# Normalising attention outputs in place of probabilities, and preparing the last branch's weights ahead

## The chip, the core and the metric

The kernel runs on one core of a Trainium2 chip. A core has five engines that run side by side, each with a queue that is worked off in order: TensorE (PE, matrix products into PSUM), VectorE (DVE), ScalarE (ACT), GpSimd (POOL) and SyncE (SP, which here issues nearly all DMAs). They meet through semaphores. The metric is the time of one execution in microseconds (us) on the device.

## What is computed

One layer on 512 tokens of width 1024: a gated feed-forward block (inner width 2816), a mixing block, and a second feed-forward block. The mixing block has two attention branches of 8 heads with 64 columns each. Branch b ("moba") attends to all keys up to the query, since with two blocks of 256 keys its choice of blocks leaves none out. Branch a ("dsa") attends to the 128 best keys by a separate score. Cut to what matters:

```python
h = h + 0.5 * swiglu(rmsnorm(h, g1), w_gu1, w_down1)
u = rmsnorm(h, g_mix)
# per head and query block, branch a; branch b is alike without the selection
logits = q @ k.T * scale + bias
p = softmax(logits)                  # exp(l - max) / sum
out = p @ v
...
mixed = sigmoid(g_a) * (out_a @ w_branch_dsa) + sigmoid(g_b) * (out_b @ w_branch_moba)
h = h + mixed @ w_out
h = h + 0.5 * swiglu(rmsnorm(h, g2), w_gu2, w_down2)
```

## The kernel before

Everything is float32. For matrix products each operand is split into a high part (rounded to the matrix engine's own 32-bit format) and a low part (the rest), and each product is made of three: high x high, high x low, low x high (`mm3`, lines 118 to 120). Activations lie transposed, 128 features on the partitions and 512 tokens along a row.

*Weights* come in units of up to 128 x 1024. `wunit` issues one DMA from SP into a tile `raw`; ScalarE makes the high part `whi` (line 108), and another engine the low part `wlo` (line 109), GpSimd but for the very first units. There are three tiles of each kind, so a load waits until the split of three units earlier is done, and a high part until TensorE has used the unit of three earlier.

*Order.* TensorE's order is written out by hand in the program. On the other engines a planner orders the instructions at build time by their place in the program and its own estimate of when each can run; those in a block with raised priority (`HURRY`) go first. From then on each queue is fixed.

*Attention* runs over 32 steps for each branch: 8 heads times 4 blocks of 128 queries, step i being head i // 4, block i % 4, with 128 to 512 keys. In a step `logits` makes the scores in PSUM (`s`), VectorE adds the bias and takes the extremum (line 589), ScalarE takes the exponential and its sum along a row (`log_exp`, line 75), VectorE makes the reciprocal of the sum (line 592) and scales the probabilities (line 593). Two steps later `turn` transposes them on TensorE, 128 x 128 at a time, into a PSUM tile `pt`, of which there are two (line 601); ScalarE copies the high part out (line 609) and VectorE the low part (line 610). After each head `values` multiplies with v into PSUM `o` and adds the two halves into `osum` (lines 626, 627); after the second head of a pair `osum` is split into high and low and is one of the four tiles of `outs`. Between these TensorE works on the filler: the projections of other heads and the gates, one k-step of three matmuls at each `yield`. Branch b's attention runs first, from about 420 to 536 us, then its output projection and the choice of the 128 keys (on VectorE), then branch a's attention, about 604 to 722 us.

*The last branch* (the loop over c below attention's end) makes, for each of 8 tiles of the output, the product of `oa` with `wb_a` (12 matmuls), times the gate (line 747), plus branch b's part (line 748), and splits the sum into high and low (lines 145, 146). Gate tiles 0 to 6 are made in attention's filler, tile 7 in the loop's first round. Behind the loop come two units of `w_out` side by side on all eight `mixed` tiles (`ps2`), then the other six.

Of the kernel before, what the change touches and what calls it, by code (L numbers as in the profile page):

```python
# [14 lines left out]
ALU = mybir.AluOpType  # L15
# [35 lines left out]
def block_kernel(ctx, tc, x, gains, wgu1, wd1, w_in, w_v, wb_a, wb_b, w_out, wgu2, wd2, rel_bias, onehot, out):  # L51
# [55 lines left out]
    def wsplit(raw, hi, lo, eng=nc.gpsimd):  # L107
        nc.scalar.activation(hi, raw, AF.Copy)  # L108
        eng.tensor_sub(lo, raw, f32(hi))  # L109

    def wunit(src):
        raw, hi, lo = wtiles(src.shape[1])
        nc.sync.dma_start(raw, src)
        wsplit(raw, hi, lo)
        return tuple(a.rearrange("p (k c) -> p k c", c=P) for a in (hi, lo))

    def mm3(pt, wh, wl, xh, xl, start, stop):
# [235 lines left out]
        while late:  # L353
            late.pop(0)[1]()

    def unit(src, xs, post):
        p = mmps()
        for _ in mmk(p, wunit(src), xs):
            tick()
            yield  # L360
        post(p)
# [62 lines left out]
    for low in lows:  # L424
        for e in range(2):
            nc.gpsimd.memset(f32(low)[HALF[1 - e], e, :], 0.0)
    turns = [0]

    def k_post(p, gain, dst):

# [110 lines left out]
            nc.gpsimd.memset(f32(pts[i][j])[:, 1408:1536], 0.0)  # L541

    sums = {}

    def attention(br, pairs, outs, extra):

        sel = br == 0
        bias, prob, tms, osum = {}, {}, {}, {}

        def table(hd):  # L550
            if hd < 8:
# [19 lines left out]
        def logits(i):  # L571
            if i >= 32:
                return
            hd, qt = divmod(i, 4)
            if qt == 1:
                table(hd + 1)
            e = hd % 2
            (q, f, _), (k, kl), _ = pairs[hd // 2]
            W = P * (qt + 1)
            N = max(W, 256)  # L580
            p = sps()
            qb = q[:, e, qt * P:(qt + 1) * P]
            nc.tensor.matmul(p[:, 0:N], qb, k[:, e, 0:N], start=True, stop=False)
            nc.tensor.matmul(p[:, 0:N], qb, kl[:, e, 0:N], start=False, stop=True)
            addend(i + 1)
            pe = tms.pop(i)
            st = T("st", 8, (P, 4))
            with tc.high_priority(HURRY):
                sums[i] = nc.vector.tensor_tensor_reduce(  # L589
                    out=pe, in0=p[:, 0:W], in1=pe, scale=f[:, 2 * qt + e:2 * qt + e + 1], scalar=3e38, op0=ALU.add, op1=ALU.min, accum_out=st[:, 0:1])  # L590
                log_exp(pe, pe, AF.Exp, bias=st[:, 0:1], scale=-1.0, accum_out=st[:, 1:2])
                nc.vector.reciprocal(st[:, 2:3], st[:, 1:2])
                nc.vector.tensor_scalar(pe, pe, st[:, 2:3], None, op0=ALU.mult)  # L593
            prob[i] = pe

        def turn(i):
            hd, qt = divmod(i, 4)
# [14 lines left out]
        def values(hd):  # L612
# [12 lines left out]
            with tc.high_priority(HURRY):  # L625
                nc.scalar.activation(ot[0:DH, :], po[DH:P, :], AF.Copy)
                nc.vector.tensor_add(osum[0][e * DH:(e + 1) * DH, :], po[0:DH, :], ot[0:DH, :])
            if e == 1:
                outs.append(split(pair_a(), osum[0]))

        table(0)
# [5 lines left out]
        for i in range(32):  # L637
            logits(i + 2)
            yield 1
            turn(i)  # L640
            yield 1
            if i % 4 == 1 and i > 4:
                values(i // 4 - 1)
            if extra and i % EVERY == 0:
                extra.pop(0)()
            yield 1
# [29 lines left out]
            keep[gi] = g1  # L676
        return proj(U_G + gi, post)

    def branch(wb, c, o, post):
        return unit(wb[c], o, post)  # L680

    def opened(gi):
        g1 = gates.pop(gi)
# [55 lines left out]
    run(fill)  # L739
    flush()  # L740
    mixed = []
    for c in range(KD):
        if c + GATES < KD:
            run(gate(c + GATES, gates))
        g1 = opened(c)
        ma = tmp()
        run(branch(wb_a, c, oa, lambda p: nc.vector.tensor_mul(ma, p, g1)))
        nc.vector.tensor_add(ma, ma, mixb[c])
        if c < 3:
            m = T("kqk"[c], 2, (P, 2, S), F32R)  # L750
# [10 lines left out]
        xs2.append(norm_tile(c, G_N2, ss3))  # L761

    ps2 = [mmps() for _ in range(2)]
    together([mmk(p, wunit(w_out[c]), mixed) for c, p in enumerate(ps2)])
    for c, p in enumerate(ps2):
        wout_post(c, p)
    for c in range(2, KD):
# [64 lines left out]
```

## Time and profile before

| | |
|---|---|
| median of 3 runs | 1164.97 us (1162.73 to 1166.91) |
| profiled execution | 1167.82 us, of which the span 1166.0 us |
| mean granted TensorE clock | 0.992 |
| TensorE, VectorE, ScalarE, GpSimd busy | 98%, 60%, 40%, 46% of the span |
| DMA | 109.59 MB, 94 GB/s on the mean |

The span goes from the first to the last instruction. Busy shares are over the whole span; the stages differ much, and a share of VectorE of 60% is made of the feed-forward blocks with less and of attention with more. TensorE's matmuls overlap (one of 512 columns is shown with some 0.39 us and they start 0.23 us apart), so a busy TensorE says that it has work, not how fast that goes. Where the clock is granted in part, its mean over a stretch is given as a share of full speed.

### The profile page before, as it was taken

To read this page: it belongs to the slowest core of one execution; us is meant where nothing else is said; L and a number is where in the kernel's file an instruction comes from. 1 tells how busy PE (TensorE), PEld (TensorE's weight loads), DVE (VectorE), ACT (ScalarE), POOL (GpSimd) and SP (SyncE) were. 2 spreads that over 40 slices of the span, in tenths; PEclk is the share of its full clock that TensorE was granted. 3 is DMA by queue.
4 is the path that set the end of the run, shared out by engine and by line. 5 is a ranking of instruction groups with operands and counts; after the bars stand their busy time and mean duration, and the time that the engine had idled before them with its cause. 6 is when DMAs were issued, how large, how long until landed. Compare 5 with 4: busy or idle time off the path is not lost.

```text
span 1166.0 us, 14074 instructions
## 1 busy us (share of the span) xinstructions
PE 1141.1 (98%) x5356; PEld 949.4 (81%) x5356; DVE 701.4 (60%) x1075; ACT 467.3 (40%) x757; POOL 532.8 (46%) x284
## 2 busy tenths in 40 slices
PE   9999999999999999999998899999999999999998
PEld 7878888888888888778887778788888888888887
DVE  5863166513556579899979986664754156622551
ACT  6322132222334668757247656433332132222221
POOL 3444444444444655753453422444444444444442
PEclk9999999999999999999999999999999999999999
DMA  7232222332323221221241311322333222332222
GB/s 235 93 111 91 99 100 91 97 102 91 99 81 110 97 76 55 92 68 69 89 137 46 100 55 35 106 104 73 108 102 98 92 107 91 94 105 91 97 84 91
DMA packets 38171, 109.59 MB, mean 94 GB/s; under 512 B 4214, under 2 KB 8664, under 8 KB 38104
## 3 DMA queue, kind: packets, MB, share of 16 engines
q1 hardware_dynamic: 37960, 108.67, 28.2%
q8 instruction: 42, 0.69, 0.2%
q14 instruction: 25, 0.20, 0.1%
q10 hardware_dynamic: 144, 0.02, 0.0%
HBM read 106.54 MB, written 2.14 MB: 93 GB/s over the span
## 4 chain that ended last, share of the span: by engine, by line
PE 83%; DVE 9%; ACT 3%; issue 3%; POOL 1%; DMA 0%; SPq 0%; POOLq 0%; ACTq 0%; DVEq 0%
PE mm L120 20%; PE mm L118 20%; PE mm L119 20%; PE s L118 7%; PE s L119 7%; PE s L120 7%; DVE l L566 1%; DVE l L589 1%; POOL wlo L109 1%; DVE l L593 1%; DVE pt L610 1%; PE pt L601 1%; ACT l L75 1%; DVE low L453 1%; PE o L620 1%
## 5 line engine op out<-in xcount | busy, mean ns | idle before, releaser
L109 POOL TENSOR_TENSOR wlo<-raw,whi 128x1024 fp32r<-128x1024 f32 (+2 forms) x199 | 466.2, 2344 | 541.4 <-ACT whi L108 536.4
L108 ACT ACTIVATE whi<-raw 128x1024 fp32r<-128x1024 f32 (+2 forms) x207 | 205.0, 992 | 520.5 <-PE mm L119 289.6
L118 PE MATMUL mm<-x,whi 128*128 128x512 f32 x632 | 253.0, 400 | 0.7 <-ACT whi L108 0.7
L120 PE MATMUL mm<-x,wlo 128*128 128x512 f32 x632 | 247.6, 392 | 0.0
L119 PE MATMUL mm<-x,whi 128*128 128x512 f32 x632 | 247.3, 391 | 0.0
L119 PE MATMUL mm<-a,whi 128*128 128x512 f32 (+1 forms) x462 | 178.7, 387 | 0.3
L118 PE MATMUL mm<-a,whi 128*128 128x512 f32 (+1 forms) x462 | 178.7, 387 | 0.0
L120 PE MATMUL mm<-a,wlo 128*128 128x512 f32 (+1 forms) x462 | 178.5, 386 | 0.0
L120 PEld LDWEIGHTS mm<-x,wlo 128*128 128x128 f32 x632 | 119.1, 188 | 25.9 <-DVE wlo L109 0.4
L118 PEld LDWEIGHTS mm<-x,whi 128*128 128x128 f32 x632 | 119.5, 189 | 23.1 <-ACT whi L108 1.5
L118 PE MATMUL s<-x,whi 128*128 128x512 f32 x352 | 137.0, 389 | 0.6 <-ACT tmp L75 0.6
L120 PE MATMUL s<-x,wlo 128*128 128x512 f32 x352 | 137.0, 389 | 0.0
L119 PE MATMUL s<-x,whi 128*128 128x512 f32 x352 | 136.9, 389 | 0.0
L119 PEld LDWEIGHTS mm<-x,whi 128*128 128x128 f32 x632 | 119.5, 189 | 21.0 <-issue 0.5
L271 DVE SCALAR_TENSOR_TENSOR h<-mm,h 128x512 f32<-128x512 f32 (+1 forms) x49 | 33.3, 680 | 165.3 <-PE mm L120 165.3
L262 DVE TENSOR_TENSOR tmp<-tmp,tmp 128x512 f32<-128x512 f32 x44 | 99.0, 2250 | 29.6 <-ACT tmp L75 29.4
L146 DVE TENSOR_TENSOR a<-tmp,a 128x512 fp32r<-128x512 f32 x49 | 88.5, 1807 | 31.9 <-ACT a L145 31.8
L119 PEld LDWEIGHTS mm<-a,whi 128*128 128x128 f32 x462 | 86.9, 188 | 18.7 <-DVE a L146 1.1
L118 PEld LDWEIGHTS mm<-a,whi 128*128 128x128 f32 x462 | 86.9, 188 | 17.6
L120 PEld LDWEIGHTS mm<-a,wlo 128*128 128x128 f32 x462 | 86.8, 188 | 17.6
L118 PEld LDWEIGHTS s<-x,whi 128*128 128x128 f32 x352 | 66.1, 188 | 14.6 <-ACT tmp L75 1.0
L120 PEld LDWEIGHTS s<-x,wlo 128*128 128x128 f32 x352 | 66.1, 188 | 13.8
(167 smaller groups left out, 1417.0 us busy)
## 6 DMA issues: line engine op xcount, KB each, us to landing
raw<-in_ffn_w_gu_dram SPq DMA_DIRECT2D x84, 512.0 KB, 3.5
raw<-in_w_in_dram SPq DMA_DIRECT2D x35, 512.0 KB, 3.5
raw<-in_ffn_w_down_dram SPq DMA_DIRECT2D x32, 512.0 KB, 3.5
raw<-in_ffn_w_down_dram SPq DMA_DIRECT2D x16, 384.0 KB, 3.0
bias<-fd SPq DMA_DIRECT2D x16, 256.0 KB, 3.5
raw<-in_w_v_dram SPq DMA_DIRECT2D x8, 512.0 KB, 3.4
raw<-in_w_out_dram SPq DMA_DIRECT2D x8, 512.0 KB, 3.5
h<-in_x_dram SPq DMA_DIRECT2D x8, 256.0 KB, 4.6
```

The source lines that it names most:

```text
L75: op = after([group["load"]], lambda: nc.scalar.activation(*a, **k))
L108: nc.scalar.activation(hi, raw, AF.Copy)
L109: eng.tensor_sub(lo, raw, f32(hi))
L118: nc.tensor.matmul(pt, wh, xh, start=start, stop=False)
L119: nc.tensor.matmul(pt, wh, xl, start=False, stop=False)
L120: nc.tensor.matmul(pt, wl, xh, start=False, stop=stop)
L146: nc.vector.tensor_sub(lo, src, f32(hi))
L262: nc.vector.tensor_mul(g1, g1, s)
L271: nc.vector.scalar_tensor_tensor(h[c][:, b], pd, 0.5, h[c][:, b], op0=ALU.mult, op1=ALU.add)
L453: nc.vector.scalar_tensor_tensor(low[h1, e, :], y[h1, :], g, f32(k)[h1, e, :], op0=ALU.mult, op1=ALU.subtract)
L566: nc.vector.scalar_tensor_tensor(tms[i], b, inv, work[:, WOFF[qt]:WOFF[qt] + W], op0=ALU.mult, op1=ALU.add)
L589: sums[i] = nc.vector.tensor_tensor_reduce(out=pe, in0=p[:, 0:W], in1=pe, scale=f[:, 2 * qt + e:2 * qt + e + 1], scalar=3e38, op0=ALU.add, ...
```

## The change

The probabilities are no longer divided by their sums. The sums of the eight steps of a pair of heads are collected in a tile `tot` of 128 x 8 (queries on the partitions). After the seventh step's `turn` (i % 8 == 6), `norms` takes the reciprocals of all eight columns, transposes them on TensorE (a 128 x 128 tile, zero but for eight columns), copies the eight rows out with the query order turned round, writes them to DRAM as a row and reads them back, each head's 512 values spread over the 64 partitions of its half. When both heads' outputs stand in `osum`, it is multiplied by that tile, on GpSimd, or on VectorE for the last pair of branch a.

In the last branch gate 7 is made ahead of the loop. The units of `wb_a` and the first two of `w_out` are prepared by `fetch`, two units ahead in the program's order, with the low part on VectorE in place of GpSimd. The other six units of `w_out` stay as they were.

```diff
--- before.py
+++ after.py
@@ -108,10 +108,10 @@
         nc.scalar.activation(hi, raw, AF.Copy)
         eng.tensor_sub(lo, raw, f32(hi))
 
-    def wunit(src):
+    def wunit(src, eng=nc.gpsimd):
         raw, hi, lo = wtiles(src.shape[1])
         nc.sync.dma_start(raw, src)
-        wsplit(raw, hi, lo)
+        wsplit(raw, hi, lo, eng)
         return tuple(a.rearrange("p (k c) -> p k c", c=P) for a in (hi, lo))
 
     def mm3(pt, wh, wl, xh, xl, start, stop):
@@ -353,9 +353,9 @@
         while late:
             late.pop(0)[1]()
 
-    def unit(src, xs, post):
+    def unit(src, xs, post, w=None):
         p = mmps()
-        for _ in mmk(p, wunit(src), xs):
+        for _ in mmk(p, w or wunit(src), xs):
             tick()
             yield
         post(p)
@@ -424,7 +424,7 @@
     for low in lows:
         for e in range(2):
             nc.gpsimd.memset(f32(low)[HALF[1 - e], e, :], 0.0)
-    turns = [0]
+    turns = [0, 0]
 
     def k_post(p, gain, dst):
 
@@ -541,11 +541,15 @@
             nc.gpsimd.memset(f32(pts[i][j])[:, 1408:1536], 0.0)
 
     sums = {}
+    recips = [cp.tile([P, P], F32, name=f"recip{i}") for i in range(2)]
+    rows_d = [dr.tile([8, P], F32, name=f"row{i}") for i in range(2)]
+    for r1 in recips:
+        nc.gpsimd.memset(r1, 0.0)
 
     def attention(br, pairs, outs, extra):
 
         sel = br == 0
-        bias, prob, tms, osum = {}, {}, {}, {}
+        bias, prob, tms, osum, tot, inv_s = {}, {}, {}, {}, {}, {}
 
         def table(hd):
             if hd < 8:
@@ -585,13 +589,31 @@
             addend(i + 1)
             pe = tms.pop(i)
             st = T("st", 8, (P, 4))
+            if i % 8 == 0:
+                tot[hd // 2] = T("tot", 2, (P, 8))
+            s1 = tot[hd // 2][:, i % 8:i % 8 + 1]
             with tc.high_priority(HURRY):
                 sums[i] = nc.vector.tensor_tensor_reduce(
                     out=pe, in0=p[:, 0:W], in1=pe, scale=f[:, 2 * qt + e:2 * qt + e + 1], scalar=3e38, op0=ALU.add, op1=ALU.min, accum_out=st[:, 0:1])
-                log_exp(pe, pe, AF.Exp, bias=st[:, 0:1], scale=-1.0, accum_out=st[:, 1:2])
-                nc.vector.reciprocal(st[:, 2:3], st[:, 1:2])
-                nc.vector.tensor_scalar(pe, pe, st[:, 2:3], None, op0=ALU.mult)
+                log_exp(pe, pe, AF.Exp, bias=st[:, 0:1], scale=-1.0, accum_out=s1)
             prob[i] = pe
+
+        def norms(pr):
+
+            r1 = recips[turns[1] % 2]
+            row = rows_d[turns[1] % 2]
+            turns[1] += 1
+            nc.vector.reciprocal(r1[:, 0:8], tot.pop(pr))
+            p = tps()
+            nc.tensor.transpose(p[:, 0:P], r1, ident)
+            o = p[0:8, P - 1:P]
+            rw = T("rw", 2, (8, P))
+            nc.scalar.activation(rw, bass.AP(o.tensor, o.offset, [list(o.ap[0]), [-1, P]]), AF.Copy)
+            nc.sync.dma_start(row, rw)
+            rb = inv_s[pr] = T("rb", 2)
+            for e in range(2):
+                a = row[4 * e:4 * e + 1, :]
+                nc.sync.dma_start(rb[HALF[e], :], bass.AP(a.tensor, a.offset, [[0, DH], [1, S]]))
 
         def turn(i):
             hd, qt = divmod(i, 4)
@@ -626,6 +648,8 @@
                 nc.scalar.activation(ot[0:DH, :], po[DH:P, :], AF.Copy)
                 nc.vector.tensor_add(osum[0][e * DH:(e + 1) * DH, :], po[0:DH, :], ot[0:DH, :])
             if e == 1:
+                eng = nc.vector if sel and hd == 7 else nc.gpsimd
+                eng.tensor_mul(osum[0], osum[0], inv_s.pop(hd // 2))
                 outs.append(split(pair_a(), osum[0]))
 
         table(0)
@@ -638,6 +662,8 @@
             logits(i + 2)
             yield 1
             turn(i)
+            if i % 8 == 6:
+                norms(i // 8)
             yield 1
             if i % 4 == 1 and i > 4:
                 values(i // 4 - 1)
@@ -676,8 +702,8 @@
             keep[gi] = g1
         return proj(U_G + gi, post)
 
-    def branch(wb, c, o, post):
-        return unit(wb[c], o, post)
+    def branch(wb, c, o, post, w=None):
+        return unit(wb[c], o, post, w)
 
     def opened(gi):
         g1 = gates.pop(gi)
@@ -739,12 +765,24 @@
     run(fill)
     flush()
     mixed = []
+
+    ahead = [wb_a[c] for c in range(KD)] + [w_out[c] for c in range(2)]
+    ready = []
+
+    def fetch():
+        if ahead:
+            ready.append(wunit(ahead.pop(0), nc.vector))
+
+    for c in range(GATES, KD):
+        run(gate(c, gates))
+    for _ in range(2):
+        fetch()
     for c in range(KD):
-        if c + GATES < KD:
-            run(gate(c + GATES, gates))
         g1 = opened(c)
         ma = tmp()
-        run(branch(wb_a, c, oa, lambda p: nc.vector.tensor_mul(ma, p, g1)))
+        w = ready.pop(0)
+        run(branch(wb_a, c, oa, lambda p: nc.vector.tensor_mul(ma, p, g1), w))
+        fetch()
         nc.vector.tensor_add(ma, ma, mixb[c])
         if c < 3:
             m = T("kqk"[c], 2, (P, 2, S), F32R)
@@ -761,7 +799,7 @@
         xs2.append(norm_tile(c, G_N2, ss3))
 
     ps2 = [mmps() for _ in range(2)]
-    together([mmk(p, wunit(w_out[c]), mixed) for c, p in enumerate(ps2)])
+    together([mmk(p, w, mixed) for p, w in zip(ps2, ready)])
     for c, p in enumerate(ps2):
         wout_post(c, p)
     for c in range(2, KD):
```

## Rows read from the trace of the kernel before

**Rows 1.** The page's first part: busy time, share of the span, instructions.

```profile
PE 1141.1 (98%) x5356; PEld 949.4 (81%) x5356; DVE 701.4 (60%) x1075; ACT 467.3 (40%) x757; POOL 532.8 (46%) x284
```

**Rows 2.** TensorE's waits: instruction and releaser, us in total, times, longest.

```profile
PE pt L601 <- DVE pt L610: 12.0, 10, 2.6
...
PE mm L118 <- DVE tmp L747: 1.5, 1, 1.5
PE mm L120 <- POOL wlo L109: 1.3, 1, 1.3
```

**Rows 3.** Busy us of each engine, sum of the six stretches named below.

```profile
sum 79.00, PE 64.31 PEld 50.98 DVE 76.41 ACT 55.38 POOL 33.76; mean PE 10.72 PEld 8.50 DVE 12.73 ACT 9.23 POOL 5.63
```

**Rows 4.** The same stretches, lines 592 and 593 alone; then their groups in attention.

```profile
sum 79.00, DVE 3.05; mean DVE 0.51
...
sum 79.00, DVE 10.13; mean DVE 1.69
...
L592 DVE RECIPROCAL st<-st 128x1 f32<-128x1 f32 x64 | 10.0, 157 | 9.0 <-ACT l L75 8.4
...
L593 DVE TENSOR_SCALAR l<-l,st 128x512 f32<-128x512 f32 x16 | 7.7, 483 | 0.2
```

**Rows 5.** Stretches: engines' busy us (instructions), granted clock, DMA share, GB/s.

```profile
529.00:538.00 9.00, 8.33 (x55) 7.84 (x54) 8.19 (x22) 7.05 (x14) 2.32 (x1) 0.81 0.11 32
664.00:676.00 12.00, 9.37 (x39) 7.70 (x38) 9.32 (x21) 6.78 (x16) 2.23 (x3) 0.72 0.18 66
751.00:763.00 12.00, 9.25 (x28) 6.76 (x26) 9.75 (x8) 3.79 (x5) 5.51 (x3) 0.72 0.32 108
```

**Rows 6.** Timeline, 674 to 688 us: start, duration, instruction, [idle before, releaser].

```profile
675.63 2.40 POOL L109 TENSOR_TENSOR wlo<-raw,whi 128x1024 fp32r<-128x1024 f32 x1 [6.57 <-ACT whi L108]
675.70 2.36 DVE L415 TENSOR_TENSOR fq<-fq 128x8 f32<-128x8 f32 x1
...
685.64 2.54 DVE L593 TENSOR_SCALAR l<-l,st 128x256 f32<-128x256 f32 x1
685.66 2.36 POOL L109 TENSOR_TENSOR wlo<-raw,whi 128x1024 fp32r<-128x1024 f32 x1 [0.67 <-ACT whi L108]
```

**Rows 7.** Timeline of the last branch, 735 to 752 us.

```profile
735.12 0.39 PE L118 MATMUL mm<-a,whi 128*128 128x512 f32 x1
...
737.84 0.39 PE L118 MATMUL mm<-a,whi 128*128 128x512 f32 x1
...
739.07 0.69 DVE L146 TENSOR_TENSOR q<-tmp,q 128x512 fp32r<-128x512 f32 x1 [0.70 <-ACT q L145]
...
739.68 0.68 DVE L747 TENSOR_TENSOR tmp<-mm,tmp 128x512 f32<-128x512 f32 x1
...
742.79 0.68 DVE L747 TENSOR_TENSOR tmp<-mm,g 128x512 f32<-128x512 f32 x1
...
749.39 2.39 POOL L109 TENSOR_TENSOR wlo<-raw,whi 128x1024 fp32r<-128x1024 f32 x1 [2.24 <-PE mm L119]
...
749.72 2.61 DVE L748 TENSOR_TENSOR tmp<-tmp,a 128x512 f32<-128x512 f32 x1
```

**Rows 8.** Groups by line (busy us, mean ns); a DMA (KB, us to landing).

```profile
L438 POOL TENSOR_TENSOR tmp<-tmp,tmp 128x512 fp32r<-128x512 f32 x8 | 10.9, 1361 | 0.8 <-ACT tmp L436 0.4
...
L109 DVE TENSOR_TENSOR wlo<-raw,whi 128x512 fp32r<-128x512 f32 x8 | 5.5, 684 | 0.6 <-ACT whi L108 0.6
...
bias<-fd SPq DMA_DIRECT2D x16, 256.0 KB, 3.5
```

**Rows 9.** Timeline, 472 to 474 us: a reciprocal and the transposes after it.

```profile
472.61 0.17 DVE L592 RECIPROCAL st<-st 128x1 f32<-128x1 f32 x1 [0.55 <-ACT l L75]
...
473.36 0.49 PE L601 MATMUL pt<-ident,l 128*128 128x128 f32 x3
```

**Rows 10.** Timeline: a weight load on SP and the first use of it.

```profile
422.08 0.33 SPq L113 DMA_DIRECT2D raw<-in_w_in_dram  x1
...
444.10 1.04 ACT L108 ACTIVATE whi<-raw 128x1024 fp32r<-128x1024 f32 x1
```

## The prediction

> **What bounds the kernel now.** I read the engines' shares first: TensorE is busy 98% of the span [rows 1]. So the change can win only what TensorE loses, and the next view is its own waits. They are few and have two places [rows 2]. Ten of them, 12.0 us in all, stand in front of line 601, the transposes of the probabilities, and end at a VectorE instruction: line 610, which empties the PSUM tile `pt` (there are two of it). Two more, 1.5 and 1.3 us, stand in front of the first matmuls with `w_out`. The other engines' idle time costs nothing.
>
> To see what VectorE does there I cut out the six stretches of attention in which TensorE stands still most (430 to 442, 487 to 500, 612 to 625, 638 to 652, 655 to 668, 676 to 690 us). In these 79.00 us TensorE is busy 64.31, so 14.69 us are lost, and VectorE is busy 76.41, or 97% [rows 3]. ScalarE and GpSimd have 55.38 and 33.76. VectorE is the bound of these stretches; outside of them TensorE keeps up with it.
>
> An idle TensorE also loses clock. After or around the stalls the mean granted clock is 0.81, 0.72 and 0.72 in stretches of 9, 12 and 12 us [rows 5]: 1.7 + 3.4 us of full-speed work in attention and 3.4 in front of `w_out`. A part of this is in the idle time already (TensorE stood still for 0.67, 2.63 and 2.75 us of the three); weighed with the missing clock that is 0.1, 0.7 and 0.8, so I count 4.2 for attention and 2.6 for `w_out`. What can be won is 14.7 + 4.2 = 18.9 us in attention and 2.75 + 2.6 = 5.35 us before `w_out`.
>
> **What the change removes in attention.** Each of the 64 steps loses the reciprocal (line 592) and the scaling of the probabilities (line 593). In the six stretches these are 3.05 and 10.13 us of VectorE [rows 4]. One of the scalings took 2.54 us, because it stood behind a GpSimd instruction that ran through the same time [rows 6]; its own work is no more than the 0.48 us that the 512-wide ones take on average [rows 4], so I count 2.06 us less: 11.1 us of work go, against 14.69 us of idle time. That is 76%, and it is the lower bound as long as nothing is added, because what is removed ahead of a stretch counts too: VectorE enters it with a shorter queue. The stretches hold 3.05 / 0.157, some 20 of the 64 steps [rows 4], so as much again twice over goes outside of them. The other end is 100%. I take 85%, a little below the middle, because within a stretch VectorE stays the busiest engine (76.4 - 11.1 = 65.3 us against TensorE's 64.3). Idle time won: 12.5 us; clock won, in the same share of 4.2: 3.6 us. Sum 16.1. ScalarE's exponential and its sum stay, and the transposes now wait for ScalarE directly, a shorter path by the two instructions.
>
> **What it adds in attention.** Per pair of heads (8 times), in this order:
> - A reciprocal of 128x8 and one 128x128 transpose on TensorE. Three transposes in a row take 0.49 us [rows 9], so one is at most 0.16 us of TensorE: 1.3 us in all, on the path.
> - The wait in front of that transpose. TensorE's order is written out, so it stops everything behind it: the filler's matmuls, the next logits, the next transposes. It is placed behind the transposes of step 6 of 8, and needs the exponential of step 7. At the tightest place I found, the reciprocal of step 15 ended at 472.78, the transposes of step 14 at 473.85 [rows 9], so 1.1 us are to spare; a queue on VectorE eats that. Also the new transpose takes one of the two `pt` tiles, so the next step's transposes need line 610 of the step just before. Bounds: 0, and one held VectorE instruction (2.4 us [rows 6]) less the 1.1 us, 1.3 us a place, 10 us in all. Since the queue on VectorE shrinks I stay near the lower end: 0.25 us a place, 2.0.
> - A copy of 8x128 on ScalarE and, on SP, a row to DRAM and two loads of it, spread over the partitions. The nearest row is a load of the bias, 256 KB from DRAM in 3.5 us [rows 8]: at most that for the row, which is small, and that again for the loads. SP is in order, so the weight loads behind these wait up to 7 us. They can: a weight tile whose load was issued at 422.08 was first read at 444.10 [rows 10], 22 us later, against 3.5 for a load. The product with `osum` comes three steps of 3 to 4 us after the reciprocals (some 20 steps in 79.00 us in the stretches, fewer us outside), against at most 7 us of transfer and 1 of transpose and copy, so it finds its factor there. Cost nothing; were that cover gone, GpSimd would stand at the multiply, and the weights' low parts behind it.
> - The multiply itself, 128x512 with two SBUF inputs: 7 on GpSimd at 1.36 us, 1 on VectorE at 0.68 [rows 8]. The latter lies at the end of attention behind a gate unit of TensorE work, and costs nothing. Of the seven, six run during attention, and each can hold VectorE as shown in [rows 6], where an instruction on 8 elements took 2.36 us and ended with GpSimd's weight split. Bounds: 0 and 6 x 1.36 = 8.2 us. VectorE now has slack, so I take 2.0.
>
> Attention: 16.1 - 1.3 - 2.0 - 2.0 = 10.8 us.
>
> **What it moves at the last branch.** Now the low parts of the weights are made on GpSimd while VectorE works on the gated sums. VectorE's line 748 is held by them; VectorE goes round in 3.11 us (line 747 at 739.68 and 742.79), longer than the 2.72 us that 12 matmuls take on TensorE (735.12 to 737.84) [rows 7]. The split of the first `w_out` unit runs 2.39 us from 749.39, holds line 748 for 2.61 us, and with it the next high part on ScalarE; TensorE then waits 1.5 us for line 747 and 1.3 us for the second split [rows 2]. Behind the change the splits are VectorE's. A 512-wide one takes 0.68 us there [rows 8]. A round is then four instructions of about 0.69, so 2.75 us, if the split falls into VectorE's 0.70 us wait for ScalarE [rows 7], and 3.45 us if it doesn't. In the first case VectorE keeps up, and both `w_out` units are ready within about 1 us of the end of the branch; in the second it is 5 us late by then (7 x 0.7), and the wait stays where it is. Bounds of the gain: 5.35 and 0. The wide splits of `w_out` cost some 1.4 us each in either case. I take 4.5, since the gap in VectorE's round is there to be filled. That gate 7 goes first changes nothing on TensorE, where it already did.
>
> Sum: 10.8 + 4.5 = 15.3 us. The profiled execution spans 1166.0 us and took 1167.8; the median of the three runs is 1165.0, 2.8 less. The gain is taken from the median: 1149.7, so I say 1150.
>
> **The rivals.**
> - *Everything goes.* No stall is left in either place and only the eight transposes are paid: 18.9 - 1.3 + 5.35 = 23.0 us, 1142. For it speaks that in all 64 steps some 11.1 x 64 / 20 = 36 us of VectorE work go, against 14.7 us of idle time; against it, that held instructions come in bursts, which an average doesn't show.
> - *GpSimd's multiply takes VectorE's place.* The stalls shrink by the 76% only (0.09 x 18.9 = 1.7 us less than forecast) and the six multiplies cost their full 8.2 us in place of 2.0: 15.3 - 1.7 - 6.2 = 7.4 us, 1158; without the gain at the last branch 2.9 us, 1162. For it: in [rows 6] two held instructions, 10 us apart, cost 2.4 and 2.5 us, whatever their size. Against: GpSimd is busy in 43% of the stretches [rows 3], and VectorE has some 36 us less to do in attention. The Trainium skill (Advanced Engine Details and Errata, VectorE Performance Modes) says that VectorE shares its second SBUF port with GpSimd, and that instructions of both that use it block each other. The trace agrees [rows 6, 7]; by that rule every multiply put on GpSimd speaks against the change, and the splits taken from it for it.
> - *TensorE waits for the reciprocals: slower than before.* The place is the transpose in `norms`. Its reciprocal isn't raised in priority as the steps' own instructions are. If the planner puts it behind two held instructions (4.8 us [rows 6]) the wait is 4.8 - 1.1 = 3.7 us, eight times 29.6; in place of my 2.0 that is 27.6 us more: 1177. It decides from (15.3 + 2.0 + 3.5) / 8 = 2.6 us a place. Against it: the held ones of [rows 6] are 10 us apart, not in a row.
> - *The change doesn't do what it says.* The planner may order the splits at the last branch as now, which is the bound of 0 above: 1154, inside the range.
>
> **How the numbers follow.** Forecast 0.55 (its own range 1144 to 1156), everything goes 0.15, the multiply 0.20, waiting for reciprocals 0.10. The measurement tells 0.3%, 3.5 us, from no change. Faster (below 1161.5) are the first two, and most of the third (0.12): 0.82. The third's tail and a mild form of the last (0.08 and 0.03) are within 0.3%: 0.11. Slower: 0.07. The range leaves out most of the last and the tails of the others: 1138 to 1162.
>
> **What would show it.** Right: the waits in front of the probabilities' transposes fall from 12.0 us to below 4, the granted clock stays at 1 through attention, and TensorE goes from the last branch into `w_out` with under 1 us of idle time. Wrong: waits in front of the new transposes, ended by its reciprocal; VectorE instructions of over 1.3 us that end together with the new multiplies; waits for the second `w_out` split, now on VectorE. The prediction fails as a whole if attention's stalls aren't VectorE's work but the order in which its queue holds it: then less work leaves them in place.

## The result, and the profile after

The changed kernel takes 1156.8 us (median of four runs, 1155.5 to 1157.2), the kernel before 1164.0 beside it. The ratio is 0.9932 [0.9911, 0.9954]: 7.2 us won, within the range, but half of the forecast of 15.3. The profiled execution of after spans 1155.4 us, that of before 1166.0; the latter was the slowest of its runs, so the two traces differ by 10.6 us and the medians by 7.2. A reading of the two traces accounts for the former.

Busy times of after, from the first part of the page (before: [rows 1]):

```profile
PE 1137.6 (98%) x5364; PEld 947.0 (82%) x5364; DVE 670.6 (58%) x966; ACT 468.5 (41%) x765; POOL 529.5 (46%) x283
```

VectorE lost 30.8 us of busy time and 109 instructions. TensorE got the eight new transposes and is still busy 98%. Its own waits in after (instruction and releaser, us in total, times, longest):

```profile
PE s L587 <- DVE st L596: 4.2, 2, 3.1
PE pt L623 <- DVE pt L632: 3.7, 4, 1.7
PE mm L118 <- DVE tmp L701: 1.3, 1, 1.3
...
PE pt L623 <- ACT rw L611: 0.8, 1, 0.8
PE mm L120 <- POOL wlo L109: 0.7, 1, 0.7
...
PE pt L608 <- DVE pt L632: 0.5, 2, 0.4
```

Line 623 is the probabilities' transpose (601 in [rows 2]). Its waits for VectorE fell from 12.0 to 3.7 us. The two in front of `w_out` [rows 2] are gone. The new transposes (line 608) wait only 0.5 us. But a wait of another kind is now the largest: logits (line 587) that wait for line 596, the instruction of each step which reads the logits out of PSUM.

To see where the time went I cut the whole of both attention branches, and the way into `w_out`, out of both traces (stretch, length, busy us and instructions of PE, PEld, DVE, ACT, POOL, granted clock, DMA share, GB/s). Before:

```profile
415.00:545.00 130.00, 124.52 (x720) 107.41 (x719) 116.53 (x312) 91.96 (x203) 74.56 (x55) 0.99 0.21 68
600.00:722.00 122.00, 111.57 (x604) 94.15 (x603) 103.76 (x246) 78.74 (x173) 44.62 (x27) 0.97 0.21 66
733.00:763.00 30.00, 27.25 (x108) 21.64 (x106) 23.78 (x24) 11.03 (x17) 14.12 (x8) 0.89 0.37 122
```

After:

```profile
415.00:545.00 130.00, 124.90 (x721) 107.91 (x720) 105.76 (x258) 91.86 (x204) 80.72 (x58) 0.97 0.23 76
600.00:722.00 122.00, 117.19 (x645) 99.35 (x645) 88.86 (x192) 82.22 (x182) 51.22 (x30) 1.00 0.25 81
727.00:757.00 30.00, 30.00 (x134) 24.72 (x133) 22.84 (x32) 12.48 (x18) 2.40 (x1) 1.00 0.40 132
```

TensorE's loss in a stretch is its idle time plus the length times what the clock lacks of 1 (an upper count, since the chip may have lowered the clock while TensorE stood still):

| | first attention | second attention | before `w_out` |
|---|---|---|---|
| before | 5.5 + 1.3 | 10.4 + 3.7 | 2.8 + 3.3 |
| after | 5.1 + 3.9 | 4.8 + 0.0 | 0.0 + 0.0 |

The second attention won 9.3 us and the way into `w_out` all of its 6.1. The first attention lost 2.2 us: VectorE has 10.8 us less to do in it, yet TensorE stands as long as before and its clock is lower. Together 13.2 us are won there; the new transposes take 2.3 back, and a stretch just ahead of the second attention some 2 us more. That leaves 8.9 of the spans' 10.6 us, as near as the clock's two digits allow (0.01 is 1.3 us in 130). The worst stretch of the first attention of after, and the one ahead of the second:

```profile
490.00:503.00 13.00, 9.86 (x40) 7.75 (x40) 12.94 (x27) 8.87 (x20) 7.27 (x5) 0.81 0.18 61
585.00:597.00 12.00, 9.98 (x43) 7.54 (x42) 10.82 (x20) 4.54 (x5) 4.60 (x3) 1.00 0.37 129
```

In the first TensorE stands 3.14 us, with its clock at 0.81 and VectorE busy through 12.94 of 13.00 us. In the second TensorE waits 1.3 us for line 701, a gate's instruction on VectorE, which stands among the instructions that choose the 128 keys (lines 530 and 533), and 0.7 us for GpSimd's low part of a weight (line 109).

### The profile page after: what moved, and what is told of

It is laid out like the page before. It is cut to its first block, busy times and chain, and to the rows that moved or that the text cites. A ratio compares the mean times of both kernels' runs of the same rounds, so it can differ in the third digit from the quotient of the medians.

```text
span 1155.4 us, 14050 instructions
## 1 busy us (share of the span) xinstructions
PE 1137.6 (98%) x5364; PEld 947.0 (82%) x5364; DVE 670.6 (58%) x966; ACT 468.5 (41%) x765; POOL 529.5 (46%) x283
## 4 chain that ended last, share of the span: by engine, by line
PE 84%; DVE 7%; issue 4%; ACT 3%; POOL 1%; DMA 0%; SPq 0%; ACTq 0%; POOLq 0%; DVEq 0%
PE mm L120 20%; PE mm L118 20%; PE mm L119 20%; PE s L118 7%; PE s L119 7%; PE s L120 7%; DVE l L596 1%; POOL wlo L109 1%; ACT l L75 1%; PE pt L623 1%; DVE l L570 1%; DVE pt L632 1%; DVE a L146 1%; DVE fq L416 1%; POOL os L652 1%
## 5 line engine op out<-in xcount | busy, mean ns | idle before, releaser
L109 POOL TENSOR_TENSOR wlo<-raw,whi 128x1024 fp32r<-128x1024 f32 (+2 forms) x189 | 453.0, 2399 | 538.8 <-ACT whi L108 534.6
L118 PEld LDWEIGHTS s<-x,whi 128*128 128x128 f32 x352 | 66.1, 188 | 14.7 <-ACT tmp L75 1.0
L119 PEld LDWEIGHTS s<-x,whi 128*128 128x128 f32 x352 | 66.1, 188 | 13.8
```

What stands on the lines that cost most here:

```text
L118: nc.tensor.matmul(pt, wh, xh, start=start, stop=False)
L119: nc.tensor.matmul(pt, wh, xl, start=False, stop=False)
```

## The experiments

All ratios are to the kernel before on the same chip, five rounds each, with 95% intervals of about 0.0018 to either side (2 us). Differences between two changed kernels are taken between their medians, and some of these come from different chips; the kernel before took 1164.0 to 1165.5 us on them. The theory was that attention's stalls are VectorE's work, lengthened where GpSimd holds an instruction of it; the rivals, that the order in which its queue is held makes them, and that the new factor or its reciprocal comes late.

**The two parts alone.** First part only: the last branch as before.

```diff
...
     for c in range(KD):
+        if c + GATES < KD:
+            run(gate(c + GATES, gates))
...
-        w = ready.pop(0)
-        run(branch(wb_a, c, oa, lambda p: nc.vector.tensor_mul(ma, p, g1), w))
-        fetch()
+        run(branch(wb_a, c, oa, lambda p: nc.vector.tensor_mul(ma, p, g1)))
...
-    together([mmk(p, w, mixed) for p, w in zip(ps2, ready)])
+    together([mmk(p, wunit(w_out[c]), mixed) for c, p in enumerate(ps2)])
```

> The change's first part alone: outputs are divided in place of probabilities, the last branch is as in the kernel before. The forecast's own terms put this part at 10.8 us and the other at 4.5. The traces of before and after say less for this part: TensorE's waits in the first attention (420 to 540 us) are as long as before, only those in the second shrank. If the forecast's terms hold, 1153 us. If the first attention won nothing, about half of it, 1158 to 1160.

1159.7 us, 0.9955 [0.9938, 0.9972]: 5.1 us won, where the forecast had 10.8. Second part only, on the kernel before:

```diff
-    def wunit(src):
+    def wunit(src, eng=nc.gpsimd):
...
+        w = ready.pop(0)
-        run(branch(wb_a, c, oa, lambda p: nc.vector.tensor_mul(ma, p, g1)))
+        run(branch(wb_a, c, oa, lambda p: nc.vector.tensor_mul(ma, p, g1), w))
+        fetch()
...
```

> The change's second part alone, in the kernel before: the last branch's units and two of w_out are prepared two units ahead, their low parts on VectorE; probabilities are divided as before. Forecast's term: 4.5 us of at most 5.35, so 1159.5. If the planner's order takes it back: 1164. The two parts lie in different stretches, so their gains should add up to the whole change's.

1159.7 us, 0.9953 [0.9938, 0.9969]: 5.2 us won, where the forecast had 4.5. So the branch came out as forecast, and by these two runs the shortfall lies in attention.

**Removal without replacement.** The division is left out: lines 592 and 593 of the kernel before go and nothing comes in their place.

```diff
-                nc.vector.reciprocal(st[:, 2:3], st[:, 1:2])
-                nc.vector.tensor_scalar(pe, pe, st[:, 2:3], None, op0=ALU.mult)
```

> The kernel before without its reciprocals and scalings (lines 592 and 593); nothing takes their place, so the division by the softmax sums is left out of the computation. This is what the change removes, without what it adds (transposes, DRAM rows, multiplies). If VectorE's amount of work made the stalls: the whole of attention's 18.9 us but a rest, 1147 to 1150, and the first part of the change, which adds 3 to 5 us back, lies that much above it. If the stalls come of VectorE being held by GpSimd's weight splits and of the order of its queue: removing work leaves most of them in place, 1156 to 1160, and the additions cost next to nothing.

1149.9 us, 0.9873 [0.9853, 0.9892]: 15.0 us, against the forecast's 16.1 for the removal. Its two attentions:

```profile
415.00:545.00 130.00, 126.85 (x741) 109.76 (x740) 108.18 (x272) 94.66 (x208) 78.06 (x56) 1.00 0.21 72
600.00:722.00 122.00, 119.66 (x657) 102.29 (x657) 90.82 (x191) 85.00 (x183) 47.11 (x28) 1.00 0.20 69
```

Both attentions gain, the clock is 1.00 in both, and TensorE's loss is 5.5 us in place of 20.9. What the first part of the change adds therefore costs 15.0 - 5.1 = 9.9 us, where the forecast had 5.3.

**The multiply on the other engine.** All eight products with the factor go to VectorE:

```diff
-                eng = nc.vector if sel and hd == 7 else nc.gpsimd
+                eng = nc.vector
```

> The changed kernel with all eight multiplies of the outputs on VectorE, at about 0.7 us each, none on GpSimd at 1.3 to 1.45. If GpSimd's multiplies hold VectorE (up to 8.2 us, 2.0 in the forecast): faster than the changed kernel by 1 to 4 us, since VectorE takes 4.9 us of work and is held 7 x 1.4 us less. If VectorE's amount of work is what counts: slower by 1 to 3 us. If neither: within 1 us.

1150.3 us, 0.9872 [0.9856, 0.9888]: 6.5 us better than after, though VectorE, the engine that was to be relieved, has seven instructions more. How the product stands in after (start, duration, instruction, idle time before it and releaser):

```profile
647.78 1.60 POOL L652 TENSOR_TENSOR os<-os,rb 128x512 f32<-128x512 f32 x1
...
649.41 0.63 ACT L145 ACTIVATE a<-os 128x512 fp32r<-128x512 f32 x1 [1.72 <-POOL os L652]
...
650.08 0.69 DVE L146 TENSOR_TENSOR a<-os,a 128x512 fp32r<-128x512 f32 x1 [1.59 <-ACT a L145]
```

and in this kernel:

```profile
643.34 1.34 DVE L652 TENSOR_TENSOR os<-os,rb 128x512 f32<-128x512 f32 x1
...
644.72 0.63 ACT L145 ACTIVATE a<-os 128x512 fp32r<-128x512 f32 x1 [0.33 <-DVE os L652]
```

The two instructions behind the product are those of `split`: line 145 on ScalarE makes the high part, line 146 on VectorE the low part. Both queues are in order, so while GpSimd multiplies, ScalarE stands 1.72 us and VectorE 1.59 us, with the next step's exponential and line 596 behind them. This is one of the two longest waits of this kind, of 1.6 to 1.9 us; at the other places neither engine stands longer than 0.6 us. The waits of these two lines through both attentions, first in after, then with the product on VectorE:

```profile
ACT a L145 <- POOL os L652: 5.3, 6, 1.8
...
DVE a L146 <- ACT a L145: 4.3, 4, 1.8
```

```profile
ACT a L145 <- DVE os L652: 0.8, 3, 0.3
...
DVE a L146 <- ACT a L145: 0.2, 1, 0.2
```

So there are two candidates for the 6.5 us: VectorE is held by the multiply, as the prediction had it, or ScalarE and VectorE wait in order for its result.

**The hold alone.** The products stay on VectorE, and GpSimd makes seven more at the same places that nobody reads:

```diff
-                eng.tensor_mul(osum[0], osum[0], inv_s.pop(hd // 2))
+                rb = inv_s.pop(hd // 2)
+                eng.tensor_mul(osum[0], osum[0], rb)
                 outs.append(split(pair_a(), osum[0]))
+                if not (sel and hd == 7):
+                    nc.gpsimd.tensor_mul(rb, osum[0], rb)
```

> The changed kernel with all multiplies on VectorE, as e4_mul_vector, and besides them seven multiplies of the same size on GpSimd, after the real ones, whose results nobody reads. VectorE's work and the wait for the product are those of e4_mul_vector; what is added is GpSimd's use of the port and of its own queue. If GpSimd's multiplies cost 6.5 us because they hold VectorE and push the weight splits back: 1155 to 1158. If they cost it because ScalarE and VectorE wait for their result in order (the split of osum stands in ScalarE's queue behind a slow product): within 1.5 us of 1150.3.

1151.4 us, 0.9887 [0.9867, 0.9906]: 1.1 us more than without them, within the intervals of the two. TensorE's, VectorE's and ScalarE's instructions stand in the same order in both traces. So in that order what a multiply takes on GpSimd, the hold of VectorE and the room in GpSimd's queue, is a small part of the 6.5.

**The wait alone.** The product stays on GpSimd as in after, and its split comes two steps later in the program, when the product should be done:

```diff
-                outs.append(split(pair_a(), osum[0]))
+                if hd == 7:
+                    finish()
+
+        def finish():
+            outs.append(split(pair_a(), osum[0]))
...
+            if i % 8 == 3 and i > 8:
+                finish()
```

> The changed kernel (seven multiplies on GpSimd), with the split of the product into high and low parts placed two steps later in the program. In the changed kernel ScalarE stands 5.3 us and VectorE 4.3 us in front of that split, waiting for GpSimd's product or for each other; with the multiply on VectorE it is 0.8 and 0.2. If these waits in order are what the GpSimd multiplies cost: 1150 to 1152.5, near to e4_mul_vector's 1150.3. If it is the hold of VectorE by the multiply, or GpSimd's queue: 1155 to 1157, as the changed kernel.

1154.0 us, 0.9904 [0.9885, 0.9922]: 2.8 us better than after, only part of the 6.5. Its waits of the two lines in both attentions are smaller, but not gone:

```profile
ACT a L145 <- POOL os L652: 2.9, 3, 1.3
...
DVE a L146 <- ACT a L145: 1.4, 1, 1.4
```

The later place may cost something itself. The control has the same later split with the product on VectorE:

```diff
-                eng = nc.vector if sel and hd == 7 else nc.gpsimd
+                eng = nc.vector
```

> The control of e8_split_later: the same later place of the split, with all multiplies on VectorE. e8_split_later came to 1154.0, 2.8 us under the changed kernel and 3.7 over e4_mul_vector. If the later place costs or wins nothing by itself: 1149.5 to 1151, and the 3.7 us are still GpSimd's multiplies (their hold, 1.1 us by e6_idle_mul, and what GpSimd's queue loses). If the later place does harm of its own: 1152 to 1154, and the wait in order was worth more than 2.8 us.

1153.1 us, 0.9901 [0.9881, 0.9921]: 2.8 us worse than with the split in its old place. So with the split later, GpSimd and VectorE as places of the product differ by 0.9 us, and with the split at once by 6.5. By this count the wait in order is worth 6.5 - 0.9 = 5.6 us, and what is left is of the size of the hold (1.1). Each of these differences has an uncertainty of about 2 to 3 us.

The count does not settle it, because the planner orders VectorE's and ScalarE's queues anew when the product or its split moves: the traces of after, of the product on VectorE and of the two with the later split have TensorE's instructions in the same order, but not VectorE's and ScalarE's. Since TensorE's order is the same, each of its instructions can be timed in both traces, and that shows where the gain arises. Of the 6.8 us between after and the product on VectorE, 3.2 arise between 488 and 512 us, at the worst stall, its lowered clock included. After:

```profile
489.61 1.29 POOL L652 TENSOR_TENSOR os<-os,rb 128x512 f32<-128x512 f32 x1
489.76 1.69 DVE L445 SCALAR_TENSOR_TENSOR tmp<-tmp,tmp 128x512 f32<-128x512 f32 x1
490.93 0.63 ACT L145 ACTIVATE a<-os 128x512 fp32r<-128x512 f32 x1 [0.56 <-POOL os L652]
...
492.99 0.68 DVE L146 TENSOR_TENSOR a<-os,a 128x512 fp32r<-128x512 f32 x1
```

and with the product on VectorE:

```profile
489.77 0.69 DVE L445 SCALAR_TENSOR_TENSOR tmp<-tmp,tmp 128x512 f32<-128x512 f32 x1
...
496.84 0.60 DVE L596 CUSTOM_DVE_ANT_0 l<-s,l,fq 128x384 f32<-128x384 f32 x1
...
498.38 0.64 DVE L146 TENSOR_TENSOR a<-os,a 128x512 fp32r<-128x512 f32 x1
```

Here ScalarE waits only 0.56 us for the product, and VectorE not at all in front of line 146. But the product holds line 445 by 1.0 us, and line 146 stands ahead of the line 596 for which TensorE waits (498.38 in after), where with the product on VectorE it stands behind it. The stretches with the two long waits (645 to 662 and 700 to 722 us) bring 0.4 and 1.2 us. So it is shown that the place of the product costs 6.5 us, and that an idle multiply costs 1.1 in the other order. How the 6.5 divide among the wait, the hold and the changed order is not shown: no run has the queues of after with the product on VectorE.

**Shorter holds.** On top of the product on VectorE, GpSimd's 1024-wide weight splits are cut into two of 512:

```diff
-        eng.tensor_sub(lo, raw, f32(hi))
+        n = raw.shape[1]
+        if eng is nc.gpsimd and n > 512:
+            for b in (slice(0, 512), slice(512, n)):
+                eng.tensor_sub(lo[:, b], raw[:, b], f32(hi)[:, b])
+        else:
+            eng.tensor_sub(lo, raw, f32(hi))
```

> The changed kernel with all multiplies on VectorE, as e4_mul_vector, and GpSimd's weight splits of 1024 columns cut into two instructions of 512: as many columns, but a VectorE instruction that is held can get in after 1.2 us in place of 2.4. If the holds by GpSimd's splits make the stalls that are left in attention (some 10 us of lost TensorE time, VectorE's held instructions cost 8 and 11 us in the two attentions): 2 to 5 us faster than e4_mul_vector's 1150.3. If it is only VectorE's amount of work: within 1 us of it. If GpSimd's second half follows without a gap that VectorE can use, or its own start costs: the same or slower by 1 to 2.

1144.6 us, 0.9827 [0.9808, 0.9846]: 5.7 us better, with no work removed. A cut might also change the order that the planner finds. In the traces it doesn't: TensorE's, VectorE's and ScalarE's instructions stand in the same order with and without it, and on GpSimd only four other instructions come ahead of a split's last half. The control makes as many pieces but cuts unevenly, which leaves nearly the old hold:

```diff
-            for b in (slice(0, 512), slice(512, n)):
+            for b in (slice(0, n - 32), slice(n - 32, n)):
```

> As e5_halves, but GpSimd's splits are cut into 992 and 32 columns in place of 512 and 512: the same number of instructions, the same order of VectorE, ScalarE and TensorE as in e5_halves, but a hold is again as long as in e4_mul_vector. If e5_halves won its 5.7 us by shorter holds: 1149 to 1151.5. If it won by another order of the queues: 1144 to 1146.

1148.6 us, 0.9857 [0.9836, 0.9878]: the uneven cut wins 1.6 us, within the intervals, and the halves 4.1 more. TensorE's, VectorE's and ScalarE's order is again the same, so the 4.1 come with the shorter hold; where the 1.6 come from is not shown. The same place in both timelines, first with halves, then uneven:

```profile
488.56 2.56 POOL L112 TENSOR_TENSOR wlo<-raw,whi 128x512 fp32r<-128x512 f32 x2 [1.41 <-ACT whi L108]
488.64 1.24 DVE L420 TENSOR_TENSOR fq<-fq 128x8 f32<-128x8 f32 x1
...
489.80 0.55 DVE L637 TENSOR_TENSOR pt<-pt,pt 128x384 fp32r<-128x384 f32 x1
```

```profile
490.55 2.33 POOL L112 TENSOR_TENSOR wlo<-raw,whi 128x992 fp32r<-128x992 f32 x1 [2.02 <-ACT whi L108]
490.72 2.19 DVE L420 TENSOR_TENSOR fq<-fq 128x8 f32<-128x8 f32 x1
```

VectorE's instruction on eight elements ends when GpSimd's current instruction ends: after 1.24 us with halves, 2.19 us without. With halves, VectorE then empties `pt` while the second half still runs.

**Shorter holds in the kernel before.** The same cut, without any part of the change:

```diff
-        eng.tensor_sub(lo, raw, f32(hi))
+        if eng is nc.gpsimd and n > 512:
+            for b in (slice(0, 512), slice(512, n)):
...
```

> The kernel before with GpSimd's splits in two halves of 512. If TensorE's stalls before came of VectorE's work in bursts that the holds make (2 to 2.4 us each): 1157 to 1161, a gain of 4 to 8 us. If VectorE was too full for that to matter: 1163 to 1165.

1150.9 us, 0.9878 [0.9857, 0.9899]: 14.6 us, about twice the most that was expected, and as much as removing the division altogether. TensorE's, VectorE's and ScalarE's order is the same as before here too. VectorE's 1075 instructions, 701.4 us before, now take 605.0:

```profile
PE 1133.9 (99%) x5356; PEld 946.2 (82%) x5356; DVE 605.0 (53%) x1075; ACT 466.9 (41%) x757; POOL 607.1 (53%) x467
```

The two attentions and the way into `w_out`, to be held against those of before above:

```profile
415.00:545.00 130.00, 126.20 (x739) 109.60 (x738) 117.53 (x325) 94.68 (x208) 81.42 (x70) 1.00 0.22 72
600.00:722.00 122.00, 116.54 (x633) 99.18 (x633) 103.11 (x251) 83.28 (x180) 46.87 (x38) 0.99 0.20 65
725.00:755.00 30.00, 29.30 (x128) 23.68 (x127) 19.95 (x24) 11.70 (x18) 15.83 (x12) 1.00 0.36 123
```

VectorE is as busy in the attention stretches as before (117.53 and 103.11 us), and TensorE loses 10.5 us in place of 20.9 there, and 0.7 in place of 6.1 on the way into `w_out`. So some 10 us of the 14.6 are attention's, and VectorE's share of busy time was no proof that the work itself was the bound: a held instruction counts as busy. With the order unchanged, each VectorE instruction can be compared with itself in the two traces, against what its shape usually takes. By this estimate the time that VectorE is held in the two attentions falls only from 29.6 to 23.5 us, but instructions held by over 1.5 us go from nine to none.

**The small instructions moved.** The four instructions on 128x8 of the chain that was seen held (lines 414 to 417) go to GpSimd, on top of the product on VectorE:

```diff
-            nc.vector.scalar_tensor_tensor(b, w, EPS, y, op0=ALU.add, op1=ALU.mult)
-            nc.vector.tensor_mul(b, b, y)
...
+            nc.gpsimd.tensor_scalar(b, w, EPS, None, op0=ALU.add)
+            nc.gpsimd.tensor_mul(b, b, y)
+            nc.gpsimd.tensor_mul(b, b, y)
...
```

> The changed kernel with all multiplies on VectorE, as e4_mul_vector, and the four small instructions on 128x8 of each q unit (lines 414 to 417) on GpSimd, as seven small ones there. In every trace so far one of them is held for 2.0 to 2.4 us by a weight split about once a unit, with the attention's own instructions behind it in VectorE's queue. If these holds make the stalls that are left: 2 to 4 us faster than 1150.3. If the next two-input instruction is held in its place, or GpSimd's longer chain makes the scores' factor late: the same or slower.

1158.2 us, 0.9943 [0.9926, 0.996]: 7.9 us worse. The waits of TensorE at the probabilities' transposes (3.7 us with the chain on VectorE), and of VectorE for the chain:

```profile
PE pt L626 <- DVE pt L635: 6.1, 4, 3.1
```

```profile
DVE fq L421 <- POOL fq L420: 7.6, 6, 2.1
```

What VectorE no longer does it now waits for, in order. That these waits are the whole of the 7.9 us is not shown.

**Quarters.** Cuts of 256 in place of 512, with the product on VectorE:

```diff
-        if eng is nc.gpsimd and n > 512:
-            for b in (slice(0, 512), slice(512, n)):
+        if eng is nc.gpsimd and n > 256:
+            for b in [slice(i, i + 256) for i in range(0, n, 256)]:
```

> As e5_halves, in quarters of 256 columns. If what is left (18 us of lost TensorE time, 9 of it in attention) still has to do with holds, 1141 to 1144; GpSimd's splits then take some 0.5 us longer each, which nobody waits for but where a unit is late. If holds of 1.2 us are already hidden: 1144 to 1147.

1141.7 us, 0.9797 [0.9776, 0.9819]. This is the best version, some 23.6 us (2.0%) below the kernel before and 15 below after. Its two attentions:

```profile
415.00:545.00 130.00, 128.14 (x750) 111.42 (x750) 107.81 (x278) 95.64 (x213) 87.60 (x101) 1.00 0.26 82
600.00:722.00 122.00, 121.11 (x665) 103.55 (x664) 92.02 (x206) 85.35 (x183) 46.42 (x56) 1.00 0.24 78
```

TensorE stands 1.9 and 0.9 us in them, at full clock.

## Why the prediction was half right

**What could be won, and the removal: right.** The forecast had 18.9 us of loss in attention and 16.1 of it won by the removal; the kernel without the division won 15.0. The rival by which everything goes is refuted by the loss that is left: 13.8 us in the two attentions of after.

**The multiply: the step that failed.** It was priced by one effect, the hold of VectorE: "Bounds: 0 and 6 x 1.36 = 8.2 us. VectorE now has slack, so I take 2.0." It cost 6.5 us by the kernel with the product on VectorE, inside the bounds but three times the value taken, and the hold by itself doesn't make it. Of its factor the prediction asked whether it is there in time, and of its result it asked nothing: it named what would stand if the factor were late, not what stands until the product is made. But the next two instructions in program order are line 145 on ScalarE and line 146 on VectorE, both in order. A multiply of 1.45 us on the mean that starts only when its sum is ready makes them stand: the places in attention show 5.3 and 4.3 us of waiting, and an idle multiply 1.1 us in the kernel's time. The later product also changed the order in which the planner put these two lines and the next steps' work, and nearly half of the difference between the traces lies where this order differs and the wait is short. So the term was mis-sized, 2.0 for 6.5; that the wait for the result is a part of it is seen, its share against the changed order is open. The diff beside the trace of before could have told the wait: the split stands right behind the product, and a 512-wide product takes 0.68 us on VectorE against 1.36 on GpSimd [rows 8].

The Trainium skill (Advanced Engine Details and Errata, VectorE Performance Modes) says that VectorE's second SBUF port is shared with GpSimd, so that GpSimd's instructions and VectorE's two-port ones block each other. The trace agrees, with the 1.24 and 2.19 us above; but of the multiplies' cost such a block, by the idle multiplies, was the small part.

**The rival of the multiply: right time, wrong mechanism.** "GpSimd's multiply takes VectorE's place" gave 1158 us and 1156.8 were measured. It got there by the full hold, 8.2 us, which the idle multiplies with their 1.1 us don't bear out. The agreement is one of size alone, and luck.

**Transposes, reciprocals, row through DRAM.** The eight transposes take 2.3 us in place of 1.3: one alone is 283 ns, not the third part of three in a row. The rival that TensorE waits for the reciprocals is refuted: the waits in front of the new transposes are 0.5 us in all, and end at line 632, not at a reciprocal. The row is cheap, as forecast: its loads landed 2.9 us after their issue.

```profile
L608 PE MATMUL pt<-ident,recip 128*128 128x128 f32 x8 | 2.3, 283 | 0.5 <-DVE pt L632 0.5
...
rb<-row SPq DMA_DIRECT2D x16, 128.0 KB, 2.9
```

What is left of the additions is 9.9 - 6.5 = 3.4 us, against 1.3 + 2.0 in the forecast. The sum is about right, its terms are not: some 2 us lie where the prediction looked for nothing, between the attentions at 585 to 597 us, in the waits for lines 701 and 109. The kernel before and the one without the division have no idle time there; the first part alone has 2.0 us:

```profile
PE mm L118 <- DVE tmp L701: 1.4, 1, 1.4
```

**The last branch: right.** Forecast 4.5, measured 5.2. The forecast hung on whether the split falls into VectorE's wait for ScalarE. It does; the round in after, starts and durations on VectorE:

```profile
734.09 0.69 DVE L784 TENSOR_TENSOR tmp<-mm,tmp 128x512 f32<-128x512 f32 x1 [0.25 <-PE mm L120]
...
735.90 0.68 DVE L109 TENSOR_TENSOR wlo<-raw,whi 128x512 fp32r<-128x512 f32 x1
...
737.29 0.68 DVE L784 TENSOR_TENSOR tmp<-mm,g 128x512 f32<-128x512 f32 x1
...
739.53 0.69 DVE L784 TENSOR_TENSOR tmp<-mm,g 128x512 f32<-128x512 f32 x1 [0.35 <-PE mm L120]
```

From line 784 to the next one are 3.20 and 2.24 us, 2.72 on average, which is TensorE's own pace [rows 7]; VectorE waits for TensorE in front of the first and the last of them (0.25 and 0.35 us), no longer the other way round.

**The signs.** Waits in front of the probabilities' transposes were to fall below 4 us: for VectorE they are 3.7, with 0.8 for the new copy on ScalarE 4.5. The clock was to stay at 1 through attention: it does in the second (1.00), not in the first (0.97). Into `w_out` TensorE doesn't stand at all. Of the signs of being wrong, the new multiplies do hold VectorE in places, as line 445 above.

**The sentence that the prediction would fail by.** "If attention's stalls aren't VectorE's work but the order in which its queue holds it: then less work leaves them in place." Both are true in part. Less work took 15.0 us, so it was work; cutting the holds took some 10 us of attention's loss with the work and the order left as they were, so it was the holds, too. Of the 20.9 us of loss, less work left 5.5 and shorter holds 10.5. The reading that fits both is that a stall needs a long hold and a long queue behind it. The worst stall of after has both:

```profile
492.92 0.16 DVE L415 TENSOR_TENSOR fq<-fq 128x8 f32<-128x8 f32 x1
493.07 2.87 POOL L109 TENSOR_TENSOR wlo<-raw,whi 128x1024 fp32r<-128x1024 f32 x1 [2.17 <-DVE fq L415]
493.60 2.37 DVE L416 SCALAR_TENSOR_TENSOR fq<-fq 128x8 f32<-128x8 f32 x1
...
498.38 0.60 DVE L596 CUSTOM_DVE_ANT_0 l<-s,l,fq 128x384 f32<-128x384 f32 x1
...
499.05 0.80 PE L587 MATMUL s<-k,q 128*128 128x512 f32 x1 [3.14 <-DVE st L596]
```

Line 415 takes 0.16 us; line 416, of the same shape, is held and takes 2.37. Five instructions that are ahead of line 596 in VectorE's order follow, and TensorE stands 3.14 us.

**What stays open.** By the parts, 15.0 - 9.9 + 5.2 = 10.3 us; the medians of the whole give 7.2. The two parts' ratios multiply to 0.9908, just below the lower end of the whole's interval, so this may be scatter, or the two parts may spoil each other's order of the queues. The wait for line 701 doesn't speak for the latter, since the first part alone has it. By the product on VectorE the first part's other additions come to 15.0 - (14.6 - 5.2) = 5.6 us in place of 3.4; the difference is of the same kind. And the 6.5 us of the multiply are not divided between the wait in order and the changed order.

## What to carry to other kernels

Before an instruction is moved to a slower engine, look at the next instruction of each in-order engine that reads its result: it may have to stand, with everything behind it, or be given another place in its queue. Here the move cost 6.5 us. A busy share that contains held instructions is not work; see how long an instruction takes against its own shortest duration, and cut what holds it before removing work. Cutting GpSimd's long two-input instructions in two made GpSimd busy for 9 us more in attention (74 us in the whole kernel), and won as much here as removing 64 reciprocals and scalings.

## What the chip showed that was not expected

VectorE's instructions on 128x8, of 0.16 us by themselves (line 415 at 492.92), can last until GpSimd's current two-input instruction ends: 2.36 us beside one of 1024 [rows 6], 2.37 and 2.19 beside ones of 1024 and 992, 1.24 beside 512. So the length of a single GpSimd instruction, not the sum of its work, sets how long one of VectorE is held. Not every instruction is: line 637, which reads PSUM, took 0.55 us from 489.80 while GpSimd's second half ran until 491.12. In the kernel before, two instructions of 512 in place of one of 1024 won 14.6 us of 1165 with the same data and the same order of TensorE's, VectorE's and ScalarE's queues; with the product on VectorE, halves won 5.7 and quarters 8.5.
